# Attention with held projection blocks and scores three row pairs ahead, in a two-layer hybrid decoder trunk on one core

## The chip, the core and the metric

One core of a Trainium2 chip runs the whole program once per execution. The metric is the time of one execution in device microseconds (us); three runs of the kernel before are known. TensorE multiplies matrices and transposes, and writes to PSUM banks; VectorE, ScalarE and GpSimd work element by element; SyncE issues the DMAs here. The profile calls them PE (PEld for its weight loads), DVE, ACT, POOL and SP. Each engine works through its own queue in order, and waits for the others by semaphores.

## What is computed

Two layers over 1024 tokens of width 1024, in float32. Each layer projects its input, runs 8 heads of forgetting attention (64 wide) and 4 retention heads (128 wide), projects their outputs back, and ends in a squared-ReLU MLP of width 4096, with a layer norm after each half. The change touches the attention heads alone:

```python
scores = jnp.einsum('bqhd,bkhd->bhqk', q_i, k).astype(jnp.float32) * scale
bias = c_i[..., :, None] - c[..., None, :]
logits = jnp.where(causal, scores + bias, -jnp.inf)
p = jax.nn.softmax(logits, axis=-1)
return jnp.einsum('bhqk,bkhd->bqhd', p.astype(v.dtype), v)
```

Here `c` is the running sum of the logarithms of the forget gates. Queries and keys are columns of the input projection (`fq`, `fk`).

## The kernel before

**Precision.** A float32 operand is split into two reduced parts, `hi` and `lo` (`split`, L159 to L165: ScalarE casts `hi`, VectorE subtracts for `lo`), and a product is three matmuls (`mm3`, L229 to L234).

**Stages of a layer.** Values and forget logits are projected first; then retention; then queries and keys of head pair 0 (`project_qk`, L469). Then comes the attention stage with its own pool, then the output projection with its norm, and the MLP in two halves. Only the attention stage concerns us; it runs twice, once per layer.

**Projection blocks.** `project_qk(l, p, ...)` makes queries and keys of heads 2p and 2p+1. It has four blocks: fq and fk, each for two halves of the tokens. A block is 24 matmuls of 512 columns into a bank of `ps_mm` (tile `mm`, two banks), followed by the eviction into `ev` (ScalarE and VectorE) and two writes to `q_d` or `k_d` in HBM (L483), one for each head. A block counts nine steps, a pair 36 (`QK_STEPS`). Pairs 1 to 3 and eight transposes of the retention output (`ret_transposes`) are the `work` that is placed between pieces of attention.

**Attention.** A head has four steps qq = 0 to 3, each two rows of 128 queries (a row pair) against 256 (qq+1) keys.
- `load(h)` brings queries `qs`, keys `ks0` and `ks1` (four DMAs, L505) and values `vp` from HBM, two buffers each; `load_bias(h)` brings the forget sums `ncb` (one buffer), and `bias` makes `rel` from them on GpSimd (L522), one buffer for each qq.
- `front(h, qq)` makes the scores. A chunk of up to 512 columns is two matmuls (L541) in one of two banks `qk`, with a mask matmul (L545) on the diagonal; VectorE evicts it with the bias and keeps the running minimum in `mx` (L547). ScalarE takes the exponential (L553), VectorE the reciprocal of the sum (L555), and GpSimd multiplies (`sc`, L556).
- `back(h, qq)` transposes these rows on PE (L569, tile `tr`, two banks), which ScalarE and VectorE split into `pt`.
- `values` multiplies with the values (L591, tile `pv`), five tiles behind (`LAG`); at the end of a pair of steps ScalarE and VectorE evict `ot` (L604, L605) and, for each odd head, `mix`.

**Order.** The loop over steps emits, for step i, the transposes of step i, the scores of step i + `DEPTH` and a number of steps of `work` that `FILL[h]` sets (`fill`, `take`), merged evenly. `need` forces what is lacking of a pair before the head that needs it is loaded. The order that is emitted isn't the order on the engines: the program is built with a scheduler that keeps a time line of its own. It puts an instruction into its engine's queue once its operands and buffers are free by that time line, and prefers what was emitted earlier. Work that depends on nothing in attention can thus be pulled forward into places where attention waits.

Of the kernel before, what the change touches and what calls it, by code (L numbers as in the profile page):

```python
# [44 lines left out]
AHEAD = 2  # L45
SC_BUFS = 4
PT_BUFS = 3
DEPTH = 2
LAG = 5
FILL = (18, 18, 18, 18, 18, 18, 4, 4)  # L50
QK_STEPS = 36


# [22 lines left out]
def hybrid_trunk(ctx: ExitStack, tc, x, w_in, w_out, w_ff1, w_ff2, ln1_g, ln1_b, ln2_g, ln2_b,  # L76
                 b_forget, ret_gn_g, cst_d, rope_d, out):
    nc = tc.nc
    A, V, G, PE, SP = nc.scalar, nc.vector, nc.gpsimd, nc.tensor, nc.sync
# [27 lines left out]
    def small(shape, tag, bufs=2):  # L107
        return sp.tile(shape, F32, tag=tag, name=nm(tag), bufs=bufs)
# [14 lines left out]
    def nm(s):  # L123
        uid[0] += 1
        return f"{s}_{uid[0]}"
# [18 lines left out]
    def tick():  # L144
        now = []
        for it in waiting:
            it[0] -= 1
            if it[0] <= 0:
                now.append(it)
        for it in now:  # L150
            waiting.remove(it)
        for it in now:
            it[1]()
# [5 lines left out]
    def split(hi, lo, src, scale=1.0):  # L159
        if scale == 1.0:  # L160
            A.copy(hi, src)  # L161
            V.tensor_tensor(lo, src, hi.bitcast(F32), op=ALU.subtract)  # L162
        else:
            A.mul(hi, src, scale)
            V.scalar_tensor_tensor(lo, src, scale, hi.bitcast(F32), op0=ALU.mult, op1=ALU.subtract)  # L165
# [58 lines left out]
    def weight(*key):  # L224
        while emitted[0] < min(ends[key[0]], place[key] + 1 + AHEAD):
            load_next()
        return loaded.pop(key)

    def mm3(ps, lhs, rhs, ks, first=True, last=True):  # L229
        n = len(ks)  # L230
        for i, k in enumerate(ks):
            for j, (a, b) in enumerate(((1, 0), (0, 1), (0, 0))):
                PE.matmul(ps, lhs(a, k), rhs(b, k), start=first and i == 0 and j == 0,  # L233
                          stop=last and i == n - 1 and j == 2)  # L234
# [231 lines left out]
            G.tensor_tensor(gt, gt, gn[:, 256 * r : 256 * r + 256], op=ALU.mult)  # L466
            defer(2, lambda tt=tt, vt=vt, gt=gt: core(tt, vt, gt))

    def project_qk(l, p, xT, pool=None):  # L469
        for name, dst, scale in (("fq", q_d, FD**-0.5), ("fk", k_d, 1.0)):  # L470
            w = weight(l, name, p)
            for hf in range(2):
                ps = ps_mm.tile([P, 512], F32, tag="mm", name=nm("mm"))
                for k in range(8):
                    mm3(ps, lambda a, k: w[a][:, k, :], lambda b, k: xT.at(b, k, 512 * hf, 512), [k], k == 0, k == 7)
                    yield
                if pool is not None and hf == 1:
                    ev = pool.tile([P, 2, 512], F32R, tag="ev2", name=nm("ev"), bufs=1)
                else:
                    ev = wp.tile([P, 2, 512], F32R, tag="ev", name=nm("ev"), bufs=1)  # L480
                split(ev[:, 0, :], ev[:, 1, :], ps, scale)
                for a in range(2):
                    SP.dma_start(dst[2 * p + a, :, :, 512 * hf : 512 * hf + 512].rearrange("s d n -> d s n").bitcast(F32),  # L483
                                 ev[64 * a : 64 * a + 64].bitcast(F32))
                tick()
                yield
# [5 lines left out]
            transpose_in(mr, t, tt, groups=1)  # L492
            yield

    def attention(pool, mixes, fill, need, take):
        pv, heads, sums, rels, pvq, outs = {}, {}, {}, {}, [], {}

        def load(h):
# [12 lines left out]
        def load_bias(h):  # L511
            ncb = pool.tile([P, S], F32, tag="ncb", name=nm("ncb"), bufs=1)
            SP.dma_start(ncb, rows(c_d[h], P))
            ref = small([P, 4], "ref")
            G.tensor_scalar(ref, ncb.rearrange("p (a b) -> p a b", b=256)[:, :, 0], -1.0, 1.0, op0=ALU.mult, op1=ALU.mult)
            sums[h] = (ncb, ref)

        def bias(h, qq):
            ncb, ref = sums[h]
            n = 256 * (qq + 1)  # L520
            rel = pool.tile([P, n], F32, tag=f"rel{qq}", name=nm("rel"), bufs=1)
            G.tensor_scalar(rel[:, 0:n], ncb[:, 0:n], ref[:, qq : qq + 1], 1.0, op0=ALU.add, op1=ALU.mult)  # L522
            rels[(h, qq)] = rel

        def front(h, qq, probs):
            qs, ks, _ = heads[h]
            n = 256 * (qq + 1)
            rel = rels.pop((h, qq))
            for rb in (2 * qq, 2 * qq + 1):
                ne = (rb + 1) * P  # L530
                sc = pool.tile([P, n], F32, tag=f"sc{qq}", name=nm("sc"), bufs=2)
                mx = None
                nw = max(ne, 256)
                cw = 512 if nw <= 512 or nw % 256 == 0 else nw // 2
                for c0 in range(0, nw, cw):
                    w = min(cw, nw - c0)
                    we = min(w, ne - c0)
                    ps = ps_qk.tile([P, 512], F32, tag="qk", name=nm("qk"))
                    last = c0 + w == nw
                    for part in range(2):  # L540
                        PE.matmul(ps[:, 0:w], qs[:, rb * P : rb * P + P], ks[part][:, c0 : c0 + w],  # L541
                                  start=part == 0, stop=part == 1 and not last)
                    if last:
                        o = rb * P - c0
                        PE.matmul(ps[:, o : o + P], ibf, mbf, start=False, stop=True)  # L545
                    m2 = small([P, 1], "mx", 6)
                    V.tensor_tensor_reduce(out=sc[:, c0 : c0 + we], in0=ps[:, 0:we], in1=rel[:, c0 : c0 + we], scale=-1.0,  # L547
                                           scalar=BIG if mx is None else mx, op0=ALU.add, op1=ALU.min, accum_out=m2)
                    mx = m2
                    if not last:  # L550
                        yield
                sm = small([P, 1], "sm", 4)
                A.activation(sc[:, 0:ne], sc[:, 0:ne], AF.Exp, bias=mx, scale=-1.0, accum_out=sm)  # L553
                ri = small([P, 1], "ri", 4)
                V.reciprocal(ri, sm)  # L555
                G.tensor_scalar(sc[:, 0:ne], sc[:, 0:ne], ri, 1.0, op0=ALU.mult, op1=ALU.mult)  # L556
                probs.append(sc)
                yield
# [61 lines left out]
        def fronts(st, probs):  # L620
            h, qq = st
            return (2 * (1 + qq // 2), front(h, qq, probs))
# [3 lines left out]
        load_bias(0)  # L626
        for j in range(DEPTH + 1):
            bias(*steps[j])
        for j in range(DEPTH):
            merge([fronts(steps[j], probs[steps[j]])])  # L630
        for i, st in enumerate(steps):
            h, qq = st
            n = fill(h, qq)
            if h + 1 < FH:
                if qq == 0:
                    if h % 2 == 1:
                        need((h + 1) // 2)
                    load(h + 1)
                if qq == 3 - DEPTH:
                    load_bias(h + 1)  # L640
            gens = [(2 * (qq + 1), back(h, qq, probs[st]))]
            if i + DEPTH < len(steps):
                nx = steps[i + DEPTH]
                gens.append(fronts(nx, probs[nx]))
            if n:
                gens.append((n, take(n)))
            merge(gens)
            if i + DEPTH + 1 < len(steps):
                bias(*steps[i + DEPTH + 1])
# [3 lines left out]
    def layer(l, xT, nxt):  # L653
# [42 lines left out]
        mix = {}  # L696
        mr = Tokens(act, "act")
        with tc.tile_pool(name=f"p2_{l}", bufs=1, reuse_waits="tile") as pool:
            def rest():
                for p in range(1, FH // 2):  # L700
                    yield from project_qk(l, p, xT, pool)
                yield from ret_transposes(mr, pool)

            work = rest()

            done = [0, 0.0]

            def fill(h, qq):
                done[1] += FILL[h] * (qq + 1) / 10
                return max(0, int(done[1]) - done[0])  # L710

            def take(n):
                for _ in range(n):
                    done[0] += 1
                    next(work, None)
                    yield

            def need(p):
                while done[0] < QK_STEPS * p:
                    done[0] += 1  # L720
                    next(work, None)

            attention(pool, mix, fill, need, take)
            for _ in work:
                pass

# [10 lines left out]
        with tc.tile_pool(name=f"p3_{l}", bufs=1, reuse_waits="tile") as outer:  # L737
# [3 lines left out]
            with tc.tile_pool(name=f"p3a_{l}", bufs=1, reuse_waits="tile") as pool:  # L741
# [42 lines left out]
                ps = banks(1) + banks(0)  # L784
# [9 lines left out]
                for tt in range(NT):  # L794
                    ps = bank()
# [351 lines left out]
    xT = Tokens(act, "act")  # L1147
    for l in range(L):
        nxt = Tokens(act, "act") if l + 1 < L else None
        layer(l, xT, nxt)  # L1150
        xT = nxt
# [27 lines left out]
```

## Time and profile before

| what | us |
|---|---|
| median of three runs | 2404.4 |
| lowest, highest | 2401.87, 2405.06 |
| the profiled execution | 2406.83 |
| its span, first to last instruction | 2404.8 |
| scores of layer 0, first to last eviction | 315.5 to 491.9 |
| scores of layer 1 | 1506.4 to 1680.9 |

How to read the rows that follow below: a row of stretches has the stretch in us from the span's start, its length, then busy us and the number of instructions (x) of PE, PEld, DVE, ACT and POOL, the granted TensorE clock (1.00 is full), the busy share of the DMA engines, and GB/s. A row of groups has line, engine, operation, output<-inputs with shapes, number, then busy us and mean ns of one, and idle us just before them with what ended the idle time. A row of the timeline starts with start and length in us and ends with the number of instructions merged into it. A row of DMAs ends with the size of one in KB and the median us from issue to landing. A PE record is longer than the pitch at which matmuls follow each other, so PE can be busy without a gap and still lose time.

### The profile page before, as it was taken

To read this page: it belongs to the slowest core of one execution; us is meant where nothing else is said; L and a number is where in the kernel's file an instruction comes from. 1 tells how busy PE (TensorE), PEld (TensorE's weight loads), DVE (VectorE), ACT (ScalarE), POOL (GpSimd) and SP (SyncE) were. 2 spreads that over 40 slices of the span, in tenths; PEclk is the share of its full clock that TensorE was granted. 3 is DMA by queue.
4 is the path that set the end of the run, shared out by engine and by line. 5 is a ranking of instruction groups with operands and counts; after the bars stand their busy time and mean duration, and the time that the engine had idled before them with its cause. 6 is when DMAs were issued, how large, how long until landed. Compare 5 with 4: busy or idle time off the path is not lost.

```text
span 2404.8 us, 32463 instructions
## 1 busy us (share of the span) xinstructions
PE 2361.1 (98%) x11888; PEld 1983.0 (82%) x11888; DVE 1510.0 (63%) x2703; ACT 1015.2 (42%) x1556; POOL 337.0 (14%) x469
## 2 busy tenths in 40 slices
PE   8999999999999999999999999999999999999997
PEld 8888887887888888888898888888888888888886
DVE  4655447854876667665755554588467766676557
ACT  3222246735544553434321212477274444543331
POOL 0223223500000000000202322244000000000003
PEclk9999999999999999999999999999999999999999
DMA  7465676433364458667555567664334544586664
GB/s 233 165 220 207 216 212 183 123 119 113 109 221 148 145 188 310 211 210 223 179 164 187 209 212 231 182 177 116 132 101 147 199 164 148 213 294 214 196 194 145
DMA packets 243807, 442.47 MB, mean 184 GB/s; under 512 B 26032, under 2 KB 128432, under 8 KB 235456
## 3 DMA queue, kind: packets, MB, share of 16 engines
q1 hardware_dynamic: 241344, 432.01, 55.2%
q10 hardware_dynamic: 2304, 8.39, 0.9%
q8 instruction: 94, 1.54, 0.3%
q14 instruction: 65, 0.53, 0.1%
HBM read 301.85 MB, written 138.48 MB: 183 GB/s over the span
## 4 chain that ended last, share of the span: by engine, by line
PE 88%; DMA 4%; DVE 4%; ACT 1%; issue 1%; SPq 0%; POOL 0%; DVEq 0%; ACTq 0%; POOLq 0%
PE mm L233 17%; PE qk L233 11%; PE qk L860 9%; PE tr L1070 7%; PE pv L1070 7%; PE pv L860 7%; PE qk L1070 5%; PE mm L1070 5%; PE mm L860 5%; PE tr L860 4%; PE tr L569 2%; PE qk L541 2%; PE pv L591 2%; DMA q_d<-ev 1%; PE pv L233 1%
## 5 line engine op out<-in xcount | busy, mean ns | idle before, releaser
L162 DVE TENSOR_TENSOR elo<-est,ehi 128x1024 fp32r<-128x1024 f32 x216 | 261.2, 1222 | 180.3 <-ACT ehi L161 179.4
L161 ACT CAST ehi<-est 128x1024 fp32r<-128x1024 f32 x216 | 226.7, 1054 | 343.4 <-PE pv L1070 127.5
L233 PE MATMUL mm<-whi,act 128*128 128x512 f32 (+1 forms) x608 | 187.9, 375 | 0.9 <-DVE act L162 0.5
L233 PE MATMUL qk<-whi,act 128*128 128x512 f32 (+1 forms) x608 | 186.6, 373 | 0.8 <-DVE act L162 0.8
L860 PE MATMUL qk<-xop,whi 128*128 128x512 f32 x608 | 187.3, 389 | 0.0
L161 ACT CAST whi<-wst 128x512 fp32r<-128x512 f32 (+1 forms) x140 | 115.9, 830 | 165.8 <-PE qk L233 36.0
L286 POOL TENSOR_SCALAR sd<-mv 128x1 f32<-128x1 f32 x15 | 13.9, 928 | 1211.4 <-DVE mv L283 1211.0
L860 PE MATMUL pv<-xop,whi 128*128 128x512 f32 x512 | 157.7, 389 | 0.0
L162 DVE TENSOR_TENSOR wlo<-wst,whi 128x512 fp32r<-128x512 f32 (+1 forms) x140 | 132.0, 946 | 39.2 <-ACT whi L161 38.6
L860 PEld LDWEIGHTS qk<-xop,whi 128*128 128x128 f32 x608 | 114.2, 188 | 23.6
L162 DVE TENSOR_TENSOR pt<-tr,pt 128x512 fp32r<-128x512 f32 (+1 forms) x160 | 99.7, 631 | 46.5 <-ACT pt L161 45.8
L233 PEld LDWEIGHTS mm<-whi,act 128*128 128x128 f32 x608 | 112.6, 192 | 19.7 <-ACT whi L161 0.8
L591 PE MATMUL pv<-pt,vp 128*128 128x256 f32 (+1 forms) x640 | 127.5, 302 | 0.2
L233 PE MATMUL mm<-act,whi 128*128 128x512 f32 x384 | 125.9, 396 | 0.0
L233 PEld LDWEIGHTS qk<-whi,act 128*128 128x128 f32 x608 | 110.3, 189 | 18.7 <-DVE act L162 1.0
L553 ACT ACTIVATE sc<-sc,mx 128x128 f32<-128x128 f32 (+7 forms) x128 | 99.4, 777 | 51.9 <-DVE mx L547 44.4
L860 PE MATMUL mm<-xop,whi 128*128 128x512 f32 x384 | 118.6, 390 | 1.5 <-DVE xop L162 1.5
L860 PE MATMUL qk<-xop,wlo 128*128 128x512 f32 x304 | 118.6, 390 | 0.0
L556 POOL TENSOR_SCALAR sc<-sc,ri 128x128 f32<-128x128 f32 (+7 forms) x128 | 96.8, 762 | 136.7 <-DVE ri L555 104.8
L161 ACT CAST pt<-tr 128x512 fp32r<-128x512 f32 (+1 forms) x160 | 85.8, 541 | 70.0 <-PE tr L569 67.9
L233 PE MATMUL mm<-wlo,act 128*128 128x512 f32 (+1 forms) x304 | 113.7, 374 | 0.7 <-DVE wlo L162 0.7
L860 PEld LDWEIGHTS pv<-xop,whi 128*128 128x128 f32 x512 | 96.1, 188 | 20.0
(278 smaller groups left out, 5942.8 us busy)
## 6 DMA issues: line engine op xcount, KB each, us to landing
est<-h_d SPq DMA_DIRECT2D x224, 256.0 KB, 3.6
wst<-in_w_ff_dram SPq DMA_DIRECT2D x76, 512.0 KB, 4.3
wr<-in_w_ff_dram SPq DMA_DIRECT2D x32, 1024.0 KB, 5.1
t_d<-ts SPq DMA_DIRECT2D x32, 1024.0 KB, 4.2
h_d<-hs SPq DMA_DIRECT2D x32, 1024.0 KB, 5.5
est<-t_d SPq DMA_DIRECT2D x128, 256.0 KB, 4.0
h_d<-rest SPq DMA_DIRECT2D x32, 768.0 KB, 5.7
est<-in_w_ff_dram SPq DMA_DIRECT2D x96, 256.0 KB, 4.8
```

The lines of the kernel that those rows point to most:

```text
L161: A.copy(hi, src)
L162: V.tensor_tensor(lo, src, hi.bitcast(F32), op=ALU.subtract)
L233: PE.matmul(ps, lhs(a, k), rhs(b, k), start=first and i == 0 and j == 0, stop=last and i == n - 1 and j == 2)
L286: G.tensor_scalar(sd, mv[:, :, 1], EPS, 1.0, op0=ALU.add, op1=ALU.mult)
L541: PE.matmul(ps[:, 0:w], qs[:, rb * P : rb * P + P], ks[part][:, c0 : c0 + w], start=part == 0, stop=part == 1 and not last)
L553: A.activation(sc[:, 0:ne], sc[:, 0:ne], AF.Exp, bias=mx, scale=-1.0, accum_out=sm)
L556: G.tensor_scalar(sc[:, 0:ne], sc[:, 0:ne], ri, 1.0, op0=ALU.mult, op1=ALU.mult)
L569: PE.transpose(tr[:, 2 * i + rb, :], probs[rb][:, j * P : j * P + P], ident)
L591: PE.matmul(ob[:, c + f * P : c + 256], vp[:, js[i], :], pt[b][:, 2 * i + f : 2 * i + 2, :], start=qq % 2 == 0 and jp == 0 and n == 0 and ...
L860: PE.matmul(ps, ops[p][a][:, k, :], right[p][b][:, k, :], start=first and k == 0 and n == 0, stop=last and k == 3 and n == 2, skip_group_c ...
L1070: PE.matmul(ps, ops[x_][:, 0, i * P : i * P + P], ops[y][:, 1, :], start=first and n == 0, stop=last and n == 2, skip_group_check=True)
```

## The change

Two numbers and one mechanism are new:
- `DEPTH` is 3 instead of 2: scores are emitted three row pairs ahead of their transposes. With it `load_bias(h + 1)`, which stood one step behind `load(h + 1)`, is emitted at the same step, qq = 0.
- `FILL` is (36, 18, 18, 18, 18, 4, 3, 3): all of pair 1 in head 0, two blocks in each of heads 1 to 4.
- Of the 12 blocks placed in the stage, the first `FREE` = 3 are as before. Before each of the others VectorE copies one element of the newest `mx` into the block's PSUM bank. The block's first matmul overwrites it, so it comes behind the copy, and the copy behind the eviction of that score chunk: the scheduler can't pull the block ahead of it.

```diff
-DEPTH = 2
+DEPTH = 3
 LAG = 5
-FILL = (18, 18, 18, 18, 18, 18, 4, 4)
+FILL = (36, 18, 18, 18, 18, 4, 3, 3)
+FREE = 3
...
                 ps = ps_mm.tile([P, 512], F32, tag="mm", name=nm("mm"))
+                if held is not None:
+                    held(ps)
...
                     mx = m2
+                    latest[0] = mx
...
-                if qq == 0:
+                if qq == 3 - DEPTH:
                     if h % 2 == 1:
                         need((h + 1) // 2)
                     load(h + 1)
-                if qq == 3 - DEPTH:
                     load_bias(h + 1)
...
+            latest, count = [None], [0]
+
+            def held(ps):
+                count[0] += 1
+                if count[0] > FREE:
+                    V.tensor_copy(ps[0:1, 0:1], latest[0][0:1, :])
...
-                    yield from project_qk(l, p, xT, pool)
+                    yield from project_qk(l, p, xT, pool, held)
```

The order changes in the two attention stages only, in the same way in both. Line numbers after the change are higher by 1 to 13 (L541 becomes L544, L569 L573, L591 L595, L233 L234, L556 L560).

*The start of the stage.* On PE, from the first scores of layer 0, before (`qk` are scores, `mm` a projection block):

```order
L541 MATMUL qk_2897<-ks_2878,qs_2876 128x256
L541 MATMUL qk_2909<-ks_2878,qs_2876 128x256
L233 MATMUL mm_3296<-act_297,wlo_2808 128x512
L233 MATMUL mm_3296<-act_298,whi_2807 128x512
L233 MATMUL mm_3296<-act_297,whi_2807 128x512
```

On PE at the same place, in the changed kernel:

```order
L544 MATMUL qk_2899<-ks_2878,qs_2876 128x256
L544 MATMUL qk_2911<-ks_2878,qs_2876 128x256
L544 MATMUL qk_2899<-ks_2881,qs_2876 128x256
L548 LDWEIGHTS ibf
L548 MATMUL qk_2899<-mbf,ibf 128x128
L544 MATMUL qk_2911<-ks_2881,qs_2876 128x256
```

Before, a projection block stands between the scores of head 0; now 12 score matmuls and their masks follow each other, then the first three transposes (`tr_3004`, of `sc_2898` and `sc_2910`), and the next block comes 14 us of PE work after the first score.

On POOL in those microseconds, before (`ncb_2886` is head 0's bias row, `ncb_3008` head 1's; `sc` are rows that are normalised for the transposes):

```order
L522 TENSOR_SCALAR rel_3006<-ncb_2886,ref_2888 128x1024
L515 TENSOR_SCALAR ref_3010<-ncb_3008 128x4
L522 TENSOR_SCALAR rel_3075<-ncb_3008,ref_3010 128x256
L556 TENSOR_SCALAR sc_2896<-sc_2896,ri_2905 128x128
L556 TENSOR_SCALAR sc_2908<-sc_2908,ri_2917 128x256
```

On POOL in the changed kernel (`ncb_2990` is head 1's bias row):

```order
L525 TENSOR_SCALAR rel_2896<-ncb_2886,ref_2888 128x1024
L560 TENSOR_SCALAR sc_2898<-sc_2898,ri_2907 128x128
L518 TENSOR_SCALAR ref_2992<-ncb_2990 128x4
L525 TENSOR_SCALAR rel_3052<-ncb_2990,ref_2992 128x256
L560 TENSOR_SCALAR sc_2910<-sc_2910,ri_2919 128x256
```

Of the two rows for the first transposes one now stands ahead of head 1's bias row, the other still behind it. SyncE issues that load at the same place in both orders.

*The middle of the stage.* On PE at a score of head 4, before:

```order
L541 MATMUL qk_4275<-ks_4007,qs_4005 128x512
L541 MATMUL qk_4275<-ks_4010,qs_4005 128x512
L545 LDWEIGHTS ibf
L545 MATMUL qk_4275<-mbf,ibf 128x128
L541 MATMUL qk_4307<-ks_4007,qs_4005 128x320
L541 MATMUL qk_4307<-ks_4010,qs_4005 128x320
L569 MATMUL tr_4167<-cst,sc_4054 128x128
```

On PE at the same score in the changed kernel:

```order
L595 MATMUL pv_4329<-pt_4188,vp_3712 128x256
L544 MATMUL qk_4301<-ks_4048,qs_4046 128x320
L544 MATMUL qk_4301<-ks_4051,qs_4046 128x320
L595 MATMUL pv_4329<-pt_4206,vp_3712 128x256
L234 MATMUL mm_4245<-act_297,wlo_3394 128x512
L234 MATMUL mm_4245<-act_298,whi_3393 128x512
L234 MATMUL mm_4245<-act_297,whi_3393 128x512
```

Before, no block stands among the scores of heads 3, 4 and 5; now the second block of pair 3 (`mm_4245`) begins here. The nine held blocks stand between the scores of heads 1 and 5, `mm_3268` the first (the last of pair 1), `mm_3904` the last of pair 2 and `mm_4587` the last of pair 3.

On DVE ahead of that block, before (the scores with 384 columns of head 4) and then in the changed kernel, with the added copy:

```order
L547 ISA sc_4250,mx_4255<-qk_4251,rel_4204 128x384
L547 ISA mx_4255 128x1
L162 TENSOR_TENSOR pt_4144<-tr_4138,pt_4143 128x512
L555 RECIPROCAL ri_4184<-sm_4182 128x1
L555 RECIPROCAL ri_4201<-sm_4199 128x1
```

The changed kernel's DVE queue at these scores:

```order
L550 ISA sc_4233,mx_4238<-qk_4234,rel_4180 128x384
L550 ISA mx_4238 128x1
L559 RECIPROCAL ri_4177<-sm_4175 128x1
L707 COPY mm_4245<-mx_4238 1x1
L163 TENSOR_TENSOR pt_4207<-tr_4201,pt_4206 128x512
```

One evicted chunk and one reciprocal stand between the score and the copy that lets the block begin.

More of the change, by code (lines that the diff above doesn't have):

```diff
@@ L467, in retention, with project_qk @@
             defer(2, lambda tt=tt, vt=vt, gt=gt: core(tt, vt, gt))
-    def project_qk(l, p, xT, pool=None):
+    def project_qk(l, p, xT, pool=None, held=None):
         for name, dst, scale in (("fq", q_d, FD**-0.5), ("fk", k_d, 1.0)):
@@ L493, in ret_transposes, with attention @@
             yield
-    def attention(pool, mixes, fill, need, take):
+    def attention(pool, mixes, fill, need, take, latest):
         pv, heads, sums, rels, pvq, outs = {}, {}, {}, {}, [], {}
@@ L721, in need @@
                     next(work, None)
-            attention(pool, mix, fill, need, take)
+            attention(pool, mix, fill, need, take, latest)
             for _ in work:
```

## The prediction

> **What bounds the kernel now.** First the page:
>
> ```profile
> PE 2361.1 (98%) x11888; PEld 1983.0 (82%) x11888; DVE 1510.0 (63%) x2703; ACT 1015.2 (42%) x1556; POOL 337.0 (14%) x469
> ```
>
> PE (TensorE) bounds the whole, so the change can only earn PE time that is lost in the two attention stages. Busy time hides most of that loss, because a record outlasts the pitch at which matmuls follow each other. So I looked next at the table by stretches: a stretch of feed-forward, one of layer 1's attention with projection work in it, and one without.
>
> ```profile
> 780.00:840.00 60.00, 60.00 (x266) 49.71 (x265) 37.88 (x56) 29.27 (x44) 0.00 (x0) 1.00 0.41 145
> 1530.00:1590.00 60.00, 60.00 (x352) 50.51 (x350) 37.43 (x97) 33.25 (x67) 19.16 (x26) 1.00 0.55 160
> 1590.00:1640.00 50.00, 46.42 (x338) 38.70 (x337) 47.67 (x146) 41.78 (x91) 29.46 (x41) 1.00 0.70 196
> 1640.00:1690.00 50.00, 48.41 (x310) 40.74 (x309) 34.73 (x96) 29.95 (x66) 17.14 (x23) 1.00 0.29 78
> ```
>
> The first row gives the pitch of a 512-column matmul, 60/266 = 0.2256 us (0.00044 a column). In the third row VectorE (the third busy time) has 47.67 of 50 us and PE idles 3.58; in the second VectorE has 37.43 of 60 and PE idles nowhere. The pitch of transposes and value products is read from the timeline:
>
> ```profile
> 510.31 0.60 PE L569 MATMUL tr<-cst,sc 128*128 128x128 f32 x4
> 510.67 0.72 PE L591 MATMUL pv<-pt,vp 128*128 128x256 f32 x4
> 511.22 0.60 PE L258 MATMUL tr<-cst,rl 128*128 128x128 f32 x4
> ```
>
> Eight of them take 511.22 - 510.31 = 0.91 us, 0.114 each. Now PE's groups of the bare stretch (1590 to 1640), and the first and last of the six of the filled one (1530 to 1590):
>
> ```profile
> L591 PE MATMUL pv<-pt,vp 128*128 128x256 f32 (+1 forms) x120 | 23.3, 303 | 0.1
> L541 PE MATMUL qk<-ks,qs 128*128 128x512 f32 (+4 forms) x78 | 20.8, 356 | 0.9 <-DVE mx L547 0.8
> L569 PE MATMUL tr<-cst,sc 128*128 128x128 f32 x108 | 17.7, 278 | 2.6 <-DVE pt L162 1.7 <-POOL sc L556 0.3
> L545 PE MATMUL qk<-mbf,ibf 128*128 128x128 bf16 x27 | 6.2, 230 | 0.0
> L258 PE MATMUL tr<-cst,rl 128*128 128x128 f32 x4 | 0.6, 272 | 0.0
> ```
>
> ```profile
> L233 PE MATMUL mm<-act,whi 128*128 128x512 f32 x95 | 32.2, 398 | 0.0
> ...
> L545 PE MATMUL qk<-mbf,ibf 128*128 128x128 bf16 x16 | 3.7, 229 | 0.0
> ```
>
> A head's 24 score matmuls have 9472 columns by the code, 395 each, so 0.174 us. Bare: (120+108+4) x 0.114 + 78 x 0.174 + 27 masks x 0.056 (128 columns), and the stretch's one projection matmul, = 41.8 us of work in 50, **8.2 us lost**. Filled: 142 projection matmuls x 0.2256 + 73 value products and 69 transposes x 0.114 + 52 scores x 0.174 + 16 x 0.056 = 58.2 in 60, a loss of 3%. VectorE's groups in the bare stretch say why:
>
> ```profile
> L162 DVE TENSOR_TENSOR pt<-tr,pt 128x512 fp32r<-128x512 f32 (+1 forms) x30 | 18.5, 629 | 0.3 <-ACT pt L161 0.3
> L547 DVE CUSTOM_DVE_ANT_0 sc<-qk,rel 128x512 f32<-128x512 f32 (+5 forms) x27 | 14.4, 537 | 0.7 <-PE qk L545 0.6
> L547 DVE CUSTOM_DVE_ANT_0 sc<-qk,rel,mx 128x512 f32<-128x512 f32 (+3 forms) x13 | 8.1, 622 | 0.5 <-PE pv L591 0.2 <-PE qk L545 0.2
> L605 DVE TENSOR_TENSOR ot<-ot,pv 64x512 f32<-64x512 f32 x7 | 4.8, 679 | 0.1
> L555 DVE RECIPROCAL ri<-sm 128x1 f32<-128x1 f32 x25 | 3.7, 155 | 0.7 <-ACT sc L553 0.5
> L162 DVE TENSOR_TENSOR mix<-ot,mix 128x512 fp32r<-128x512 f32 x3 | 3.3, 1110 | 0.0
> L547 DVE DVE_READ_ACCUMULATOR2_ANT mx<- 128x1 f32 x39 | 3.2, 82 | 0.0
> L162 DVE TENSOR_TENSOR wlo<-wst,whi 128x1024 fp32r<-128x1024 f32 x1 | 1.2, 1223 | 0.0
> ```
>
> A head needs 10 pt, 8+4 score chunks, 12 maximum reads, 8 reciprocals, 2 ot and one mix: 6.3+4.3+2.5+1.0+1.2+1.4+1.1 = 17.8 us of records. These overlap (the rows add up to 57.2 us in 50), so a head takes VectorE, by estimate, 17.8 x 50/57.2 = 15.6 us. PE needs 24 x 0.174 + 8 x 0.056 + (36+40) x 0.114 = 13.3. Bare heads are thus bound by VectorE; with two projection blocks (48 x 0.2256 = 10.8) PE has 24.1 and bounds.
>
> **The change, part by part.** (1) *Spreading.* FILL gives heads 1 to 4 two blocks each, and the holds keep the scheduler from pulling them forward. VectorE's part of such a head is 17.8 + two ev (0.69 each, row below) + one wlo 1.22 = 20.4 of records, 17.8 us, against 24.1. The bare stretch's 41.8 us of work should then run at the filled loss, 3% or 1.3: gain 8.2 - 1.3 = **6.9 us a layer**; nothing if something else there makes PE late, and up to 3.7 more if heads 6 and 7 profit too (1640 to 1690: idle 1.59, and the bare stretch lost 2.3 times its idle). In layer 0 the clock also dipped in the bare stretch:
>
> ```profile
> 418.00:420.00 2.00, 0.83 (x7) 0.83 (x8) 0.43 (x4) 0.33 (x3) 2.00 (x3) 1.00 1.09 358
> 420.00:422.00 2.00, 2.00 (x13) 1.84 (x12) 1.23 (x5) 1.76 (x6) 2.00 (x3) 0.64 1.11 292
> 422.00:424.00 2.00, 2.00 (x8) 1.44 (x8) 1.46 (x6) 1.29 (x4) 1.11 (x3) 0.51 0.99 236
> ```
>
> That is 2 x 0.36 + 2 x 0.49 = **1.7 us**, behind 2 us in which PE worked 0.83; it goes with the bare stretch.
>
> (2) *The copies.* A 1x1 copy on VectorE takes 138 ns:
>
> ```profile
> L979 DVE COPY wr<-qk 1x1 f32<-1x1 f32 x32 | 4.4, 138 | 5.8 <-ACT gt L465 5.8
> ```
>
> 18 make 2.5 us, beside other work, since VectorE has 17.8 of 24.1. The copy itself waits for nothing that earlier VectorE rows haven't waited for; but all of PE's queue stands behind the block's first matmul. In the shown place (mm_4245) the score was issued some 2.8 us of PE work before the block, and VectorE has the chunk (0.54+0.08), a reciprocal 0.16 and the copy in between: 0.9 us. At the tightest block (the first held one) it is 2.2 of 2.7. I take 0; the dearest end is 1 us for each of 18.
>
> (3) *The start.* Now PE has no block between the first scores and the first transposes. Before, in layer 0:
>
> ```profile
> 310.77 0.32 SPq L513 DMA_DIRECT2D ncb<-c_d  x1
> 313.81 0.40 PE L541 MATMUL qk<-ks,qs 128*128 128x256 f32 x2
> 319.04 0.20 POOL L515 TENSOR_SCALAR ref<-ncb 128x4 f32<-128x4 f32 x1 [11.57 <-DMA ncb<-c_d]
> 319.33 0.48 POOL L522 TENSOR_SCALAR rel<-ncb,ref 128x256 f32<-128x256 f32 x1
> 319.79 0.84 POOL L556 TENSOR_SCALAR sc<-sc,ri 128x128 f32<-128x128 f32 x2
> 321.04 0.50 PE L569 MATMUL tr<-cst,sc 128*128 128x128 f32 x3
> ```
>
> GpSimd's queue is stopped until head 1's bias row (ncb) has landed, and normalises head 0's second row only then; SyncE issues that load at the same place in both orders. So the first transposes can't start before about 320.3. PE has from 313.81 until then 12 score matmuls of 4096 columns (1.8 us) and 5 masks (0.3): it loses 6.4 - 2.1 = **4.3 us**, and I take layer 1 to be alike. Before, projection filled that time. Bounds 3.5 (the three GpSimd rows a little sooner) to 6.5 (the following 11 us of PE work, with 11 chunks, 6 pt, 6 reciprocals and an ot for VectorE in them, 12.6 us of records, lose the bare 20%).
>
> (4) *Keys just in time.* Heads 2, 4 and 6 need keys that the held blocks make. From the last matmul of block 3268, 3904 and 4587 to the first score of these heads PE has, counted in the changed order, 10.3, 11.2 and 8.1 us of work. The chain beside it (eviction by ScalarE and VectorE, write to k_d, four loads of keys, which SyncE holds behind that write):
>
> ```profile
> 322.33 0.59 ACT L161 CAST ev<-mm 128x512 fp32r<-128x512 f32 x1 [1.35 <-DMA q_d<-ev]
> 322.95 0.69 DVE L162 TENSOR_TENSOR ev<-mm,ev 128x512 fp32r<-128x512 f32 x1 [0.78 <-ACT ev L161]
> k_d<-ev SPq DMA_DIRECT2D x32, 256.0 KB, 3.5
> 1534.74 1.76 SPq L505 DMA_DIRECT2D ks<-k_d  x3
> ks<-k_d SPq DMA_DIRECT2D x64, 256.0 KB, 6.7
> ks<-k_d SPq DMA_DIRECT2D x1, 256.0 KB, 4.0
> ```
>
> The last row is one load into an empty queue (issued at 1533.58), the row above the median of all. 0.59 + 0.69 + 3.5 + 1.76 + 4.0 = 10.5 us, or 13.2 with 6.7: waits of 0.2, 0 and 2.4 (2.6 a layer), or 2.9, 2.0 and 5.1 (10.0). I take **2.6**, since in the new order only the k_d write stands right ahead of these loads; the ends are 0 and 10.0.
>
> Issuing load_bias with load moves one DMA ahead on SyncE; its reader is a head away, nothing.
>
> *Sum:* 6.9 - 4.3 - 2.6 = 0.0 a layer, and 1.7 once: 1.7 us. The profiled execution took 2406.8 us (span 2404.8), so 2405.1; the median of the runs is 2404.4, 2.4 lower, so **2402.7**. A measurement here can tell about 0.2% (4.8 us): this is no change.
>
> **A rule against the change.** Layer 0's clock dipped behind 2 us in which PE stood idle for 1.17, and the start in (3) leaves it idle for 4.3 of 6.4 us. The Trainium skill ("TensorE: Matmul & The Clock Gate", section "Why this matters for your kernels") says that idle gaps above about 3 us between bursts bring back the half clock. By that rule the start costs nothing more as long as VectorE spreads the 12 scores and no gap reaches 3 us, and the sum stays. The trace disagrees: the clock fell after less than that, and the measurement decides. So the dip is a rival here.
>
> **Rivals.**
> A. *The spread pays whole.* Keys land in time (0) and the start costs 3.5: 3.4 us a layer, 8.5 in all: 2395.9. For it: the single load of 4.0. Against: the three rows of GpSimd.
> B. *Heads 6 and 7 profit too*, 3.7 a layer over the forecast: 2395.3. For it: VectorE enters them without a backlog. Against: these heads have output-projection work already.
> C. *Slower: keys late.* From median landings on, 7.4 us a layer above the forecast: 2417.5; half way 2410. For it: 6.7 is the median of 64. Against: many of those were queued behind 2 MB of other loads.
> D. *Holds wait for VectorE*, 1 us for each of 18: 2420.7. It decides once VectorE's queue is more than 2.5 us behind; against: 17.8 of 24.1.
> E. *The clock dips at the start*, 1.7 us in each layer: 2406.1.
> That the change doesn't do what it says is excluded by the order: blocks stand between heads 1 and 5.
>
> **The numbers.** Forecast 0.30, E 0.10: no change 0.40. A 0.25, B 0.13: faster 0.38. C 0.17, D 0.05: slower 0.22. The range goes from A with part of B, 2393, to half of C, 2411; the forecast's own, with (3) and (4) each a microsecond off in both layers, is 2398.7 to 2406.7.
>
> **What would show it.** PE without idle and VectorE near 75% where bare heads stood; 2 us of PE idle before the first transposes of head 0, ended by GpSimd's sc; waits of scores of heads 2, 4 and 6 for ks, 2 to 3 us a layer. It is wrong if projection's first matmuls wait for VectorE, or if the first transposes start soon after the first scores.

## The result and the profile after

| kernel | median us | lowest, highest | ratio to before (95%) |
|---|---|---|---|
| before (4 runs) | 2404.73 | 2401.87, 2405.29 | |
| changed (4 runs) | 2433.38 | 2428.16, 2434.73 | 1.0111 (1.0099 to 1.0124) |

The change costs 28.6 us, 1.1%. The forecast was 2402.7, its range 2393 to 2411: slower than any of its rivals. First the row of the core, with the span and the mean granted clock, of the kernel before:

```profile
core 0: 2404.8 us, clock 0.997
```

And of the changed one:

```profile
core 0: 2433.0 us, clock 0.992
```

The span is 28.2 us longer, and 0.8% of it instead of 0.3% is missing in the clock. At half clock that is 2 x 0.008 x 2433 = 39 us instead of 2 x 0.003 x 2405 = 14: 25 us more at half speed. PE was busy for some 20 us of that (23.3 in the eight windows that are counted below, 3.4 in the one before), so about 10 us of the loss, over a third, aren't waiting but work at half speed. The page's first part doesn't show it, since PE is just as busy at half clock:

```profile
PE 2370.4 (97%) x11888; PEld 1990.1 (82%) x11888; DVE 1502.2 (62%) x2721; ACT 1011.4 (42%) x1556; POOL 334.9 (14%) x469
```

The part that was meant to change did so. The row of stretches of the changed kernel as far into layer 1's stage as the bare one stood before (85 to 135 us behind the first score):

```profile
1606.00:1656.00 50.00, 48.77 (x304) 41.25 (x303) 33.64 (x96) 29.05 (x65) 18.90 (x26) 1.00 0.54 159
```

PE idles 1.2 us instead of 3.6, and VectorE has 33.6 us instead of 47.7. The waits of PE in layer 0's stage (312 to 512 us), with total, number and longest:

```profile
PE qk L544 <- DMA ks<-k_d: 6.8, 5, 3.2
PE tr L573 <- POOL sc L560: 2.7, 1, 2.7
PE tr L573 <- DVE pt L163: 1.8, 4, 0.7
PE qk L544 <- DVE mx L550: 1.6, 5, 0.5
PE qk L544 <- issue: 1.4, 1, 1.4
...
PE tr L573 <- DVE mm L707: 0.4, 1, 0.4
```

And in layer 1's stage (1518 to 1712 us):

```profile
PE qk L544 <- DMA ks<-k_d: 5.4, 3, 2.2
PE tr L573 <- POOL sc L560: 2.8, 1, 2.8
```

Scores that wait for keys (ks) are new and the largest; then come the first transposes, which wait for GpSimd. The held copies (`mm L707`) cost one wait of 0.4 us.

**Where the time is.** For the table I took all PE records of a trace and summed, for each matmul, the time to the next one's start less the usual pitch of its shape (0.227 us for 512 columns, 0.119 for 256, 0.109 for 128, and so on, as they stand in these traces). That is the time PE loses, to waits and to the clock alike (the useless matmuls of idle_work count as work). A row is one profiled execution. The stretches count from the first score of a stage; both layers are added. The last column counts stretches of 3.41 us at half clock between 100 and 2300 us.

| kernel | -20 to 30 | 30 to 70 | 70 to 130 | 130 to 220 | sum | half clock |
|---|---|---|---|---|---|---|
| before | 3.8 | 2.3 | 19.1 | 12.1 | 37.4 | 1 |
| changed | 18.0 | 11.2 | 7.2 | 28.4 | 64.8 | 8 |
| nohold | 6.1 | 2.2 | 18.6 | 12.0 | 38.9 | 2 |
| depth2 | 12.6 | 4.0 | 5.1 | 26.1 | 47.9 | 6 |
| free5 | 7.6 | 2.7 | 9.8 | 24.7 | 44.8 | 4 |
| keys_early | 13.5 | 3.8 | 7.9 | 12.1 | 37.2 | 1 |
| idle_work | 16.7 | 5.8 | 7.3 | 16.9 | 46.7 | 3 |
| weight_late | 18.4 | 4.4 | 2.1 | 35.7 | 60.5 | 9 |
| spread_a | 8.3 | 4.3 | 9.3 | 9.6 | 31.5 | 0 |
| spread_b | 5.4 | 3.4 | 14.6 | 17.7 | 41.1 | 1 |
| spread_d2 | 6.3 | 2.9 | 9.9 | 10.5 | 29.5 | 0 |
| spread_c | 6.9 | 2.7 | 8.8 | 21.1 | 39.5 | 1 |

The sums differ by 27.4 us between before and changed, the spans by 28.2: the table holds nearly the whole effect. The middle (70 to 130), where heads stood bare, gives back 11.9 us; the start costs 14.2, the keys of head 2 8.9, and the stretch with the keys of head 6 16.3.

**The clock.** Rows of stretches of the changed kernel, cut where its clock changes. PE's busy time is the first number behind the length, the clock the third from the end:

```profile
319.60:323.01 3.41, 0.69 (x7) 0.56 (x6) 0.85 (x6) 0.76 (x3) 1.65 (x4) 1.00 1.04 398
323.01:326.42 3.41, 3.41 (x15) 2.93 (x15) 2.41 (x8) 2.26 (x6) 2.44 (x5) 0.50 0.56 154
353.73:357.14 3.41, 1.60 (x9) 1.20 (x8) 0.17 (x1) 1.37 (x4) 1.53 (x2) 1.00 1.18 240
357.14:360.56 3.42, 2.91 (x14) 2.75 (x14) 1.91 (x7) 0.72 (x3) 0.11 (x1) 0.50 1.02 259
360.56:363.97 3.41, 3.41 (x17) 3.10 (x16) 2.30 (x7) 2.45 (x6) 0.32 (x2) 0.50 1.02 258
456.13:459.54 3.41, 1.31 (x12) 1.17 (x11) 2.78 (x8) 2.76 (x6) 2.11 (x2) 1.00 1.03 243
459.54:462.96 3.42, 1.45 (x6) 1.12 (x6) 0.00 (x0) 0.00 (x0) 0.00 (x0) 0.50 1.04 252
462.96:466.37 3.41, 3.41 (x17) 3.01 (x17) 0.97 (x6) 1.60 (x6) 1.47 (x2) 0.50 1.09 325
...
1558.64:1562.05 3.41, 2.13 (x14) 1.75 (x13) 0.40 (x2) 1.95 (x4) 1.88 (x2) 1.00 1.17 239
1562.05:1565.47 3.42, 3.42 (x29) 2.95 (x28) 3.26 (x11) 2.44 (x7) 0.37 (x1) 1.00 1.02 233
```

A window in which PE is busy for less than half (0.69, 1.60, 1.31 of 3.41 us) is followed by one at half clock; the one with 2.13 is not. The waits need not be long: around 354 us the longest was 1.4. And a window that begins at half clock and waits again (459.54) brings another. A window full of work at half clock costs up to 1.7 us. The lower speed shows in the pitch: at head 6 four transposes take from 464.18 to 465.02 us, 0.21 each, where the prediction read 0.114 at full clock:

```profile
464.18 1.05 PE L259 MATMUL tr<-cst,rl 128*128 128x128 f32 x4
465.02 0.85 PE L573 MATMUL tr<-cst,sc 128*128 128x128 f32 x3
```

**The keys of head 6.** The timeline of the changed kernel from the last block of pair 3 on: PE's last matmul of the block, the eviction by ScalarE and VectorE, SyncE's DMAs (start, and the time for which it issues), and PE at the scores of head 6.

```profile
448.01 0.40 PE L234 MATMUL mm<-act,whi 128*128 128x512 f32 x1
448.58 0.59 ACT L162 CAST ev<-mm 128x512 fp32r<-128x512 f32 x1
449.79 0.68 DVE L163 TENSOR_TENSOR ev<-mm,ev 128x512 fp32r<-128x512 f32 x1
...
450.50 1.23 SPq L486 DMA_DIRECT2D k_d<-ev  x2
452.25 0.39 SPq L212 DMA_DIRECT2D wst<-in_w_out_dram  x1
453.67 2.40 SPq L508 DMA_DIRECT2D ks<-k_d  x4
...
456.56 0.88 PE L595 MATMUL pv<-pt,vp 128*128 128x256 f32 x6
460.60 0.55 PE L544 MATMUL qk<-ks,qs 128*128 128x256 f32 x1 [3.16 <-DMA ks<-k_d]
...
462.49 0.55 PE L544 MATMUL qk<-ks,qs 128*128 128x256 f32 x1 [0.91 <-DMA ks<-k_d]
```

The DMAs issued from 440 to 464 us, with size and the median time from issue to landing:

```profile
ks<-k_d SPq DMA_DIRECT2D x8, 256.0 KB, 7.3
wst<-in_w_out_dram SPq DMA_DIRECT2D x1, 512.0 KB, 5.9
```

From the end of the block (448.4) to the first score (460.6) the chain takes 12.2 us, and PE was busy for 8.6 us of it. Of the eight loads of ks, the first four are head 6's own (issued from 453.5 to 456.1 us):

```profile
ks<-k_d SPq DMA_DIRECT2D x4, 256.0 KB, 6.4
```

They don't find an empty queue: 512 KB of weights (wst) go out 1.4 us ahead of them. One takes 6.4 us in the median, not 4.0, and the next head's, which come behind, take 7.8 to 10.2.

**The start.** Timeline of the changed kernel: SyncE, PE and GpSimd at the first scores of layer 0.

```profile
313.05 0.32 SPq L516 DMA_DIRECT2D ncb<-c_d  x1
314.63 0.40 PE L544 MATMUL qk<-ks,qs 128*128 128x256 f32 x2
...
321.27 0.20 POOL L518 TENSOR_SCALAR ref<-ncb 128x4 f32<-128x4 f32 x1 [3.05 <-DMA ncb<-c_d]
321.56 0.48 POOL L525 TENSOR_SCALAR rel<-ncb,ref 128x256 f32<-128x256 f32 x1
322.02 0.48 POOL L560 TENSOR_SCALAR sc<-sc,ri 128x256 f32<-128x256 f32 x1
...
322.55 0.55 PE L573 MATMUL tr<-cst,sc 128*128 128x128 f32 x3 [2.72 <-POOL sc L560]
```

GpSimd stands until head 1's bias row has landed, 8.1 us behind its issue, and only then normalises the second row; PE waits 2.72 us for it.

### The profile page after: what moved, and what is told of

Same layout as the page of the kernel before. It is cut to its first block, busy times and chain, and to the rows that moved or that the text cites. A ratio compares the mean times of both kernels' runs of the same rounds, so it can differ in the third digit from the quotient of the medians.

```text
span 2433.0 us, 32468 instructions
## 1 busy us (share of the span) xinstructions
PE 2370.4 (97%) x11888; PEld 1990.1 (82%) x11888; DVE 1502.2 (62%) x2721; ACT 1011.4 (42%) x1556; POOL 334.9 (14%) x469
## 4 chain that ended last, share of the span: by engine, by line
PE 85%; DMA 8%; DVE 4%; ACT 1%; issue 1%; SPq 1%; POOL 0%; DVEq 0%; ACTq 0%; POOLq 0%
PE mm L234 14%; PE qk L234 10%; PE qk L870 8%; PE tr L1080 7%; PE pv L870 7%; PE pv L1080 7%; PE qk L1080 5%; PE mm L1080 5%; PE mm L870 5%; PE tr L870 4%; PE qk L544 2%; PE tr L573 2%; DMA wr<-in_w_ff_dram 2%; PE pv L595 2%; DMA ks<-k_d 2%; DMA k_d<-ev 1%
## 5 line engine op out<-in xcount | busy, mean ns | idle before, releaser
L234 PE MATMUL mm<-whi,act 128*128 128x512 f32 (+1 forms) x608 | 187.2, 373 | 1.0 <-DVE act L163 0.5
L234 PE MATMUL qk<-whi,act 128*128 128x512 f32 (+1 forms) x608 | 186.0, 373 | 0.8 <-DVE act L163 0.8
L234 PEld LDWEIGHTS mm<-whi,act 128*128 128x128 f32 x608 | 111.8, 191 | 19.7 <-ACT whi L162 0.9
L544 PE MATMUL qk<-ks,qs 128*128 128x512 f32 (+4 forms) x384 | 110.5, 377 | 17.0 <-DMA ks<-k_d 12.1
L595 PE MATMUL pv<-pt,vp 128*128 128x256 f32 (+1 forms) x640 | 125.0, 304 | 0.7 <-ACT pt L162 0.4
L234 PEld LDWEIGHTS qk<-whi,act 128*128 128x128 f32 x608 | 110.3, 189 | 18.7 <-DVE act L163 1.0
L234 PE MATMUL mm<-act,whi 128*128 128x512 f32 x384 | 121.7, 394 | 0.0
L560 POOL TENSOR_SCALAR sc<-sc,ri 128x128 f32<-128x128 f32 (+7 forms) x128 | 95.8, 755 | 159.4 <-DVE ri L559 133.9
L234 PE MATMUL mm<-wlo,act 128*128 128x512 f32 (+1 forms) x304 | 113.3, 373 | 0.7 <-DVE wlo L163 0.7
```

What stands on the lines that cost most here:

```text
L595: PE.matmul(ob[:, c + f * P : c + 256], vp[:, js[i], :], pt[b][:, 2 * i + f : 2 * i + 2, :], start=qq % 2 == 0 and jp == 0 and n == 0 and ...
```

## The experiments

The theory (W in the texts on record): the loss is PE waiting at the start and for keys that were just made, and the half clock behind these waits. Against it: the held copies themselves (H), or three row pairs ahead (D).

**free5**

```diff
-FREE = 3
+FREE = 5
```

> FREE is 5 instead of 3, nothing else: the last block of pair 1 and the first of pair 2 may go where the scheduler likes, and its order puts them among head 0's first scores, with 6.9 instead of 2.1 us of PE work from the first score to the first transposes; the keys of head 2 come 24.6 us of work ahead of their scores instead of 10.5; head 6's lead stays 8.2. Theory W (the time went to PE waiting at the start and for keys just made, and to the half-clock stretches that follow such waits): the start gives back 2.75 us of idle and 1.7 of clock a layer, head 2 gives back 2.3 and 3.4 in layer 0 and 1.3 in layer 1; 22 us of work in heads 0 and 1 become bare and lose about 16% again, 3.5 a layer. In all 16 less and 7 more: 2424. Rival H (the held copies themselves hold PE up): two of nine copies a layer are gone, so 2/9 of 28.6, 2427, and the wait at the start stays. Rival D (three row pairs ahead cost by themselves): 2433, no change.

Measured: 2415.74 us, ratio 1.0047 (1.0035 to 1.0060). The gain of 15 to 18 us (by the ratios, and by the medians) is more than the 9 expected: the start lost 7.6 instead of 18.0 and head 2 2.7 instead of 11.2, while the new bare heads cost less than I thought. PE no longer waits for GpSimd's sc in layer 0's stage; its largest wait there is the one that stays at head 6:

```profile
PE qk L544 <- DMA ks<-k_d: 4.3, 2, 2.9
```

D, which allowed no change, is out as the whole cause; H, which gave each copy an equal share of the loss, is out too: two copies fewer of nine can't give that much.

**keys_early**

```diff
-FILL = (36, 18, 18, 18, 18, 4, 3, 3)
+FILL = (40, 20, 20, 20, 8, 4, 3, 3)
```

> FILL is (40, 20, 20, 20, 8, 4, 3, 3), nothing else: blocks a little earlier, so that the last matmul of pair 3 comes 16.3 us of PE work ahead of head 6's first score instead of 8.2, and head 4's keys 19.3 instead of 11.3; head 2's lead 11.4 and the start stay. Theory W: the wait for ks at head 6 goes (4.07 us a layer in the trace) with the two half-clock windows behind it (3.4 a layer), 15 in both layers; some 8 us more of bare heads cost 1.3 a layer: 2433.4 - 15 + 2.6 = 2421. The start's wait and its clock dip stay as they are. Rival H: nine copies as before, no change, 2433. Rival D: no change, 2433.

Measured: 2408.22 us, 1.0013 (1.0005 to 1.0022): 24 to 25 less, with all nine copies and three row pairs ahead. The stretch of head 6 lost 12.1, as before the change, instead of 28.4. I had expected 2421: the additional bare heads cost nothing that shows, and head 2 of layer 0, with 0.9 us more lead, kept its full clock. Its PE waits in layer 0:

```profile
PE tr L573 <- POOL sc L560: 2.4, 2, 2.2
PE qk L544 <- DMA ks<-k_d: 1.7, 2, 1.1
```

Some 8 us more of lead for heads 4 and 6 thus take away 16 us of the effect at head 6. The 7 us at head 2 need not come from its 0.9 us: in idle_work below head 2 lost half as much as in the changed kernel, without an edit there. H and D both said 2433.

**depth2**

```diff
-DEPTH = 3
+DEPTH = 2
```

> DEPTH is 2 again, the holds and FILL stay: leads of keys 14.8, 15.2 and 9.8 us of PE work for heads 2, 4 and 6 instead of 10.5, 11.3 and 8.2; first scores to first transposes 2.1 as with 3. Theory W: the start's loss stays, the wait at head 2 goes (7 us with its clock in both layers), head 6 waits 1.6 a layer less and may keep its clock dip: 2416 to 2424. Rival D (depth 3 costs): back to 2405. Rival H (holds cost): 2433 or more, since with a depth of 2 less work stands ahead of each hold.

Measured: 2419.77 us, 1.0063 (1.0050 to 1.0075), where W put it; with the holds the third row pair costs 12 to 14 us. In the table that is head 2 (11.2 against 4.0), whose first scores it brings nearer to their keys, and the start (18.0 against 12.6), where W had expected no change. And the wait at head 6 didn't shrink as expected. It moved to a load that stands behind the same loads of ks in SyncE's queue, the retention output (rl). PE's largest wait in layer 0's stage:

```profile
PE tr L259 <- DMA rl<-r_d: 5.0, 1, 5.0
```

**nohold**

```diff
-                    yield from project_qk(l, p, xT, pool, held)
+                    yield from project_qk(l, p, xT, pool)
```

> No held copies; DEPTH 3, FILL and the earlier bias load stay. By the order the blocks stand again in heads 0 to 2 as in the kernel before (leads 51, 56 and 44 us). Theory W: no late keys, no bare start: within 4 us of the kernel before, 2401 to 2409. Rival D (three row pairs ahead, or the new FILL, cost by themselves): well above, 2415 to 2433. Rival H: about 2405 too, so this run parts D from the others only.

Measured: 2403.32 us, 0.9997 (0.9988 to 1.0006): no change against the kernel before. DEPTH, FILL and the bias load do nothing by themselves, because the scheduler pulls the blocks forward again; D is out.

**idle_work**

```diff
                     latest[0] = mx
+                    if (h, rb, c0) == (5, 6, 448):
+                        idle_work(18)
...
+        def idle_work(n):
+            ps = ps_mm.tile([P, 512], F32, tag="mm", name=nm("idle"))
+            V.tensor_copy(ps[0:1, 0:1], latest[0][0:1, :])
+            qs, ks, _ = heads[5]
+            for k in range(n):
+                PE.matmul(ps, qs[:, 0:P], ks[0][:, 0:512], start=k == 0, stop=k == n - 1)
```

> The changed kernel with 18 more matmuls of 512 columns (4.06 us) that nobody reads, on PE right ahead of head 6's first score in each layer, where PE waits 4.07 us for ks. Theory G (half of the loss there is the clock: a stretch of 3.4 us in which PE works less than half is followed by 3.4 or 6.8 us at half clock): PE stays busy, the two half-clock windows at head 6 go, the keys come when they came; 3.4 us less a layer, 2433 - 7 = 2426, with more work than before. Rival P (only the wait costs time and the clock's dip costs nothing beside it): no gain, 2433, or up to 8 more where the added work does not fit the wait.

Measured: 2423.23 us, 1.0082 (1.0068 to 1.0096). With 8.1 us of useless matmuls more, the kernel is 7 (by the ratios) to 10 us (by the medians) faster than the changed one. PE in layer 0, in the place of the wait:

```profile
448.90 4.31 PE L635 MATMUL idle<-ks,qs 128*128 128x512 f32 x18
453.04 0.28 PE L544 MATMUL qk<-ks,qs 128*128 128x256 f32 x1
```

The keys are there when the idle work ends, the clock stays at 1.00 there, and the four half-clock windows at head 6 are gone. G had said 7, but that the whole came out near it is partly luck. In the table the stretch of head 6 loses 11.5 us less, and the useless matmuls fill 8.1 of them, so it gains 3.4, half of what G had. Head 2 gains 5.4 more (5.8 instead of 11.2), which the edit doesn't touch: in layer 0 it waited 0.8 us there and kept its clock. Theory P, by which the dip costs nothing, still doesn't fit, since the stretch does more work in less time, and the transposes above ran at about half speed.

**weight_late**

```diff
+            lim = min(lim, place[(key[0], "wo", 0, 4)])
...
                 ks.append(kt)
+            if h == 6:
+                while emitted[0] < min(ends[now[0]], place[(now[0], "fk", 3)] + 1 + AHEAD):
+                    load_next(latest[0][0:1, :])
```

> The changed kernel with the loads of the output projection's weights (wst) held back until head 6's keys are being loaded, by a copied element as for the blocks; block ends stand 9.9, 11.7 and 8.2 us of PE work ahead of the scores that need them, as before to 0.6 us. By SyncE's order no wst stands between the write of k_d and the four loads of ks for heads 2, 4 and 6 any more. Theory Q (the keys are late because their loads share the DMA engines with the wst issued just ahead: they land 5.8 to 8 us after their issue, and 4.0 on an empty queue): ks lands about 2 us sooner, head 6 waits 2 instead of 4.07 a layer and keeps at most one of its two half-clock windows, head 2 in layer 0 loses its dip: 2433 less 2 x 2 less 5 to 10 of clock, 2419 to 2424. Rival L (the landing time is the loads' own and the lead is simply too short): within 4 us of 2433.

Measured: 2429.30 us, 1.0103 (1.0089 to 1.0117): by the time, nearest to L. By place both are partly right. The DMAs issued at head 2 of layer 0 (340 to 352 us):

```profile
ks<-k_d SPq DMA_DIRECT2D x5, 256.0 KB, 4.4
```

And at head 6 (440 to 456 us):

```profile
ks<-k_d SPq DMA_DIRECT2D x8, 256.0 KB, 6.0
wst<-in_w_out_dram SPq DMA_DIRECT2D x2, 512.0 KB, 6.9
```

With no weights ahead, the keys of head 2 land in 4.4 us (head 2's own took 6.5 to 8.0 in the changed kernel), and the loss from 30 to 70 falls from 11.2 to 4.4. At head 6 the loads of wst come right behind those of ks, the wait for ks stays (3.6 us in layer 0 by the gaps of PE, 3.1 in layer 1), new waits for rl follow, and the stretch loses 35.7. What other loads are in the queue thus sets a good part of a load's time; at head 6 the experiment moved them instead of taking them away, and how short the chain is there without any was not measured.

**spread_a, spread_b, spread_c, spread_d2**: five blocks free, seven spread, with the numbers that the texts name; spread_d2 has DEPTH 2.

```diff
-DEPTH = 3
-FILL = (36, 18, 18, 18, 18, 4, 3, 3)
-FREE = 3
+DEPTH = 2
+FILL = (63, 12, 12, 12, 10, 4, 3, 2)
+FREE = 5
```

> FREE is 5 and FILL is (63, 12, 12, 12, 10, 4, 3, 2): two blocks at the start, then seven spread from 38 to 123 us of PE work behind it; keys 38.6, 37.5 and 16.7 us ahead. Theory W: no start wait, no key wait, no clock dip. From the bins of the runs with the earlier keys and with five free blocks: 3.5 us lost in the first 50 us of the stage and 10.8 in the rest, 14.3 a layer, against 18.7 in the kernel before: 2405 - 9 = 2396. Rival B (VectorE is late somewhere anyhow, since it has a little less room wherever PE has more): 2405, no change against the kernel before.

> FREE is 5 and FILL is (54, 18, 16, 14, 8, 4, 3, 3): like the last, with the blocks a little earlier in the later heads (keys 33.8, 30.4 and 25.4 us ahead) and 4 us more without projection behind the last block. Theory W: 1 us a layer more than the last, 2398. Rival B: 2405.

> FREE 5 and FILL (58, 14, 14, 14, 10, 4, 4, 2), depth 3: the seven held blocks stand 8 us apart nearly everywhere, where the best version so far has gaps of up to 11 us. Theory W: the stretches without projection that lost 1.6 and 1.5 us in its bins shrink, keys 34.8, 32.2 and 16.9 us ahead: 2 us a layer less, 2398. Rival B (evenness beyond this earns nothing): 2401, within 2 us.

> The best version so far (FREE 5, FILL (63, 12, 12, 12, 10, 4, 3, 2), measured at 2401.5) with scores two row pairs ahead instead of three; keys 41.9, 39.6 and 18.7 us ahead. Theory W: with keys and start covered, the depth only sets how much work stands between scores and transposes, and nothing waited for that: 2401, within 4 us. Rival N (three row pairs are what lets VectorE and GpSimd run late without stopping PE): slower by 1 to 2 us of waits a layer and more, 2405 to 2410.

| kernel | us | ratio to before (95%) |
|---|---|---|
| spread_a | 2401.53 | 0.9988 (0.9979 to 0.9997) |
| spread_b | 2411.80 | 1.0033 (1.0021 to 1.0046) |
| spread_c | 2409.31 | 1.0015 (1.0006 to 1.0024) |
| spread_d2 | 2400.26 | 0.9981 (0.9972 to 0.9991) |

spread_d2 beats both kernels, by 0.2%, and needs no third row pair; rival N is out. It has no key wait and no half clock in the stages. Its largest wait of PE in layer 0's:

```profile
PE qk L544 <- DVE mx L550: 1.1, 2, 0.8
```

spread_a beats the kernel before too, by about a third of what I expected, so its rival B is partly right. spread_b and spread_c miss by 14 and 11: PE waits for rl again in heads 6 and 7, with a half-clock window in layer 0 in each. PE's waits of spread_c in layer 0's stage:

```profile
PE qk L544 <- DVE mx L550: 2.8, 6, 1.0
PE tr L259 <- DMA rl<-r_d: 2.2, 1, 2.2
```

Why those loads come late with one FILL and not with the next is not settled, so the order alone doesn't carry a forecast of a few us here.

## Why the prediction was wrong

1. *Spreading, 6.9 us a layer and 1.7 once (15.5 in all)*: right in mechanism, somewhat less in size. Between 70 and 130 us the loss fell by 11.9.
2. *The copies, 0*: right. One wait of 0.4 us a layer; nohold and keys_early show that the copies matter only through the order. Rival D of the prediction is out.
3. *The start, 4.3 a layer*: mechanism right, GpSimd and the bias row. From the first score to the first transposes it took 7.9 and 6.7 us with 2.1 of work, so it lost 5.8 and 4.6, inside the bounds of 3.5 to 6.5 (2.7 and 2.8 of it in the one wait for GpSimd). With two half-clock windows, up to 3.4 us, the start lost 14.2 in both layers instead of 8.6. So rival E came with it; it had a tenth of the chances, because I took one dip of 1.7 us behind 1.17 idle in 2 us for a thing that might not return, although PE was to be idle for 4.3 of 6.4.
4. *Keys just in time, 2.6 a layer*: the step that failed, in two ways. Its size: I took 4.0 us for a load of ks, "since in the new order only the k_d write stands right ahead of these loads". That was not so. A load of weights stood there too, and SyncE's order would have told it; with it a load for head 6 took 6.4. PE's waits for the keys of heads 2, 4 and 6 were 7.1 and 5.4 us in the two layers, inside the ends of 0 to 10 and about half way to rival C's 10.0 (layer 0: 6.8 for ks less 1.1 at head 0, and the 1.4 that the profile puts down to issue, since a load of head 2's keys landed 0.1 us before that score). Its kind: C was priced as waiting alone, 2417.5. Six of the eight half-clock windows stand behind these waits. The stretches with the keys of heads 2 and 6 (30 to 70, and 130 to 220) lost 25.2 us more than before, where the sum had 5.2: 11.8 in these waits, some 8 at half clock (PE was busy for 16.5 us of the six windows); the remaining 5 are not put down to a cause.
5. *The sum*: an error in one direction. Both kinds of new wait, at the start and for keys, fall on a PE with nothing else to do, since the change took its filler away, and most of the long ones brought the clock down (head 2's in layer 1 didn't). I had the dip of layer 0 in my sum as a gain, and nowhere as a price but in E.

The rule that I weighed (dips only after gaps above 3 us) would have left the sum as it was. The decision for the measurement against it was right, but then it should have been used wherever PE waits.

## What to carry to other kernels

Price a wait of TensorE twice: the wait, and the half clock behind it if PE is busy for less than half of a window of 3.4 us. Before filler work is held back, ask what it covers where it stands, here the start and the way of the keys through HBM, and count the distance from a product's last matmul to its first reader against the whole chain with the loads that are queued around it: here 8 to 10 us were too short, 16 were enough. If the scheduler is free to undo a table of numbers, the table does nothing (nohold), and what decides is where the held work ends.

## What the runs showed of the hardware

The clock changes on a fixed grid. In the changed kernel half clock begins at 323.01, 357.14, 459.54, 1527.92 and 1661.04 us: 10, 40, 353 and 392 times 3.413 us behind the first. In the ten traces of this study that have such windows between 100 and 2300 us, what follows a window depends on how long PE was busy in it:

| clock in the window | PE busy, share of it | windows | followed by |
|---|---|---|---|
| full | below 0.52 | 21 | half clock, all |
| full | 0.52 | 2 | half clock one, full the other |
| full | 0.57 and more | all others | full |
| half | 0.29 to 0.86 | 13 | half clock, all |
| half | 0.87 | 2 | half clock one, full the other |
| half | 0.99 and more | 21 | full, all |

So at full clock the line lies near half of a window. At half clock it lies higher, near 0.87: a PE that is busy throughout gets its full clock back, and one that waits for more than about half a microsecond of the window stays slow. The Trainium skill ("TensorE: Matmul & The Clock Gate", section "What's actually happening") has a free-running window of 3413 ns, and with that the traces agree; it names an idle window as what lowers the clock, and there they differ: the one at 353.73 was busy for 1.60 of 3.41 us.

Because the grid doesn't move with the wait, a like wait dips in one place and not in another: 1.60 us of 3.41 busy at head 2 in layer 0, 2.13 in layer 1.
